# Six PSUM buffers by role for the seven products of a Strassen pair, the seventh product issued behind the next pair's first, and eight early loads at the start of attention

## The chip, the cores and the metric

The kernel runs on one core of one Trainium2 chip. The metric is device time in microseconds (us) of the whole program. The times of before are three timed runs; the profile is one further execution, taken by the hardware profiler, with its own time.

## The reference, cut to what matters

A decoder block with two branches over 2048 positions and 1024 channels, all in float32:

```python
h = rms_norm(x, g_norm) * (1 + scale) + shift
proj = h @ w_in                                     # 1024 x 8192
x_rnn, z_rnn, q, k, v, z_attn, g_r, g_a = split(proj)
xc = causal_depthwise_conv(x_rnn); hr = rg_lru(xc)  # a gated linear recurrence over positions
y_rnn  = (hr * silu(z_rnn)) @ w_out_rnn
o      = dilated_attention_mixture(rope(q), rope(k), v)
y_attn = (o * silu(z_attn)) @ w_out_attn
merged = sigmoid(g_r + b) * y_rnn + sigmoid(g_a + b) * y_attn
x = rms_norm(x + gate * (merged @ w_o), g_final)
```

## The kernel before

Every float32 operand of a matrix product is split into a high part `h` (float32r) and a remainder `l`, and a product is three matmuls, `h*h + h*l + l*h` (`mm3`, L148). ScalarE (ACT) makes the high part, GpSimd (POOL) or VectorE (DVE) the low part.

The program has these stages. Positions are handled in two halves, f = 0 and f = 1, of two 512-column chunks each.

- **Values** (`values_half`, L645): the columns of `w_in` for v, and the building of the right-hand operands B11, B21, B12, B22, T1 to T4 (`build`, L447, transposes on TensorE (PE) into a PSUM tile of the pool `pg`).
- **Pairs** (`strassen`, L312): 28 pairs of 128 output rows in each half. A pair is a 2 x 2 block product done with seven block products in place of eight, each of 4 x 3 = 12 matmuls of 128x512. In order of the code they are X (B11), Z (T2), W (T3), V (T1), X again (B21), W again (T4), V again (B22). X, W and V are written twice: the second product of each accumulates onto the first in the same PSUM tile. In between the first content is read: u1 = X (ACT, L338), u2 = Z + u1 (DVE, L339), u3 = W + u2 (DVE, L344), and `done(1, 1, V, u3)`. After the second products come `done(0, 0, X)`, `done(1, 0, W, u2)` and `done(0, 1, V, u2)`. Each `done` begins with `total` (L379), one ACT copy or one DVE addition out of PSUM (L385), and goes on with what belongs to the output: `recurrent` (L674: convolution taps, gates on PE, exponentials, root, scan), `gate_pairs` (L879), `plain_pairs` (L853) or `rotated_pairs` (L833: the rotary part of q and k, which needs tables Ct and St that `rotary_tables` makes at the start of that section). The 28 pairs are 22 of recurrent, gate and plain kind, then 2 rotated, then 4 plain ones.
- In half 0 the left operands (seven sums of blocks of `w_in`) are loaded, added on DVE (L254 to L262), split on ACT and POOL (`split_s`, L198) into a ring of seven tiles S0 to S6, used, and stored to DRAM (`sD`); in half 1 they are read back, one DMA of 512 KB for each product (`load_next`, L282), into the same ring.
- The steps of `recurrent` are not issued at once. `steps_after` (L216) puts each behind a number of further products: in units of products after the pair's `done(0, 0)`, tap 0, taps 1, split 2, gates 4, sigmoids 5, decay 6, exponentials 7, root 8, scan 9, finish and store 10; for the second column chunk 7 later.
- **Attention** (L973 on): heads in an order written out by slots. Matmuls of the output products (`steps`, L1306) fill PE between its parts; they begin the stage. Their right operands are 8 tiles yh/yl of each chunk, made by `split_y` (L1339) from rows of `yaT`. For the first chunk, k = 0 to 3 are loaded during the last pair into R0 to R3 (`load_next`, L294), and k = 4 to 7 after the split of k - 4 has released its R tile (L1371).
- **Output** (L1457 on): the last projection and the final norm.

Within the stages up to attention a scheduler decides the order in which each engine's instructions stand; `tc.high_priority()` marks the reads of PSUM. The rows of an engine stand in that order, and a row that waits holds up the rows behind it. Attention's order is that of the code.

PSUM has eight banks. Before, five are in the pool `pj` and rotate over whatever asks next (four tiles a pair, two tiles a step of values), three in `pg` (transposes of `build`, the gates of `recurrent`, the rotary tables).

In the profile the products of the pairs are the group `pj<-T,S` at L146, the DVE totals `ev`, `t`, `zs` or `xr` `<-pj,u` at L385, by the output that they belong to.

## Time and profile before

| what | value |
|---|---|
| three timed runs | 2347.64, 2355.68, 2358.10 us (median 2355.68) |
| profiled execution, its own time | 2350.21 us |
| its span, first to last instruction | 2348.4 us |
| granted TensorE clock, mean | 0.986 |
| busy share of the span | PE 95%, DVE 58%, ACT 51%, POOL 41% |

A row of a timeline reads: start, duration, engine, line, operation, output tile <- input tiles, count, and in brackets the idle time of that engine just before it and what ended it. A row of waits reads: who waited, for whom, us in total, times, longest. A row of windows reads: the stretch, its length, then busy us and the number of instructions of each engine, the granted clock of PE, the busy share of the DMA engines and GB/s. "PE busy" comes with modelled ends, so the number of matmuls in a stretch says more than its busy time.

### The profile page before, as it was taken

How to read it: one execution, taken by the hardware profiler on the slowest of the kernel's cores; microseconds unless marked ns; L12 is line 12 of the kernel's file. 1: busy time of each engine (PE TensorE's matmuls, PEld its weight loads, DVE VectorE, ACT ScalarE, POOL GpSimd, SP SyncE). 2: the span in 40 equal slices, each digit the busy share in tenths (PEclk: the TensorE clock that was granted, in tenths of full speed). 3: DMA queues.
4: the chain of work that ended last, by engine and by line, in shares of the span. 5: the costliest groups of instructions: out<-in, count | busy, mean ns of one | idle time of the engine just before them, and what ended most of it. 6: DMA issues, size and time to landing. Idle time of an engine off the chain costs nothing.

```text
span 2348.4 us, 34038 instructions
## 1 busy us (share of the span) xinstructions
PE 2228.8 (95%) x11397; PEld 1875.8 (80%) x11397; DVE 1353.7 (58%) x2457; ACT 1202.0 (51%) x2386; POOL 954.5 (41%) x734
## 2 busy tenths in 40 slices
PE   6999999999999999999999999899989998989998
PEld 6897777777777898778888877788879887978887
DVE  6837666766676534444444472366667778657443
ACT  4636656666643535555444410466667777634111
POOL 1356655655555533333111120355556656433000
PEclk9999999999999999999999999999999999999999
DMA  7376877677878659899676678888888878799532
GB/s 259 99 226 220 275 248 258 244 247 247 258 259 251 220 175 338 305 310 330 215 234 224 232 241 257 267 257 274 263 247 262 240 244 251 221 315 291 173 119 96
DMA packets 427331, 569.19 MB, mean 242 GB/s; under 512 B 71990, under 2 KB 292882, under 8 KB 426132
## 3 DMA queue, kind: packets, MB, share of 16 engines
q1 hardware_dynamic: 389316, 447.27, 61.4%
q10 hardware_dynamic: 37648, 119.70, 13.4%
q8 instruction: 90, 1.47, 0.3%
q14 instruction: 85, 0.70, 0.1%
q0 software_dynamic: 192, 0.05, 0.0%
HBM read 355.08 MB, written 211.82 MB: 241 GB/s over the span
## 4 chain that ended last, share of the span: by engine, by line
PE 62%; DMA 9%; DVE 8%; ACT 5%; issue 4%; POOL 2%; SPq 1%; ACTq 1%; DVEq 0%; POOLq 0%
PE pj L146 43%; PE pq L146 7%; PE sc L146 4%; PE o L146 4%; DMA R<-in_w_in_dram 1%; PE pg L146 1%; PE pT L1154 1%; POOL S L160 1%; DMA S<-sD 1%; PE pT L1167 1%; DMA vraw<-vN 1%; ACT L742 1%; DMA gw<-in_w_mod_dram 1%; DVE xc L718 1%; DMA R<-yaT 1%
## 5 line engine op out<-in xcount | busy, mean ns | idle before, releaser
L146 PE MATMUL pj<-T,S 128*128 128x512 f32 x4704 | 1120.6, 398 | 29.8 <-DVE ev L385 20.1
L146 PEld LDWEIGHTS pj<-T,S 128*128 128x128 f32 x4704 | 888.7, 190 | 249.6 <-DVE ev L385 27.0
L146 PE MATMUL pj<-yh,S 128*128 128x512 f32 x1024 | 370.5, 407 | 12.4 <-ACT yh L154 6.7
L160 POOL TENSOR_TENSOR S<-R,S 128x512 fp32r<-128x512 f32 x168 | 244.8, 1469 | 277.7 <-ACT S L200 105.7
L146 PEld LDWEIGHTS pj<-yh,S 128*128 128x128 f32 x1024 | 195.1, 191 | 49.6 <-ACT yh L154 7.1
L146 PE MATMUL pj<-yl,S 128*128 128x512 f32 x512 | 202.8, 396 | 1.0 <-POOL yl L160 0.6
L1070 ACT ACTIVATE pp<-pp,st 128x256 f32<-128x256 f32 (+3 forms) x256 | 133.9, 524 | 110.9 <-DVE st L1069 110.2
L146 PE MATMUL pj<-S,T 128*128 128x256 f32 x1152 | 160.7, 295 | 4.4 <-ACT S L154 1.3
L146 PEld LDWEIGHTS pj<-S,T 128*128 128x128 f32 x1152 | 150.1, 199 | 5.9 <-POOL S L160 1.6
L160 POOL TENSOR_TENSOR S<-s,S 128x512 fp32r<-128x512 f32 x84 | 112.2, 1338 | 73.9 <-ACT S L200 38.6
L163 DVE TENSOR_TENSOR ptl<-pT,pth 128x384 fp32r<-128x384 f32 (+1 forms) x160 | 97.9, 628 | 66.8 <-ACT pth L154 64.7
L1134 ACT ACTIVATE pp<-pp,M 128x256 f32<-128x256 f32 (+3 forms) x256 | 118.0, 522 | 9.0 <-DVE M L1258 9.0
L718 DVE SCALAR_TENSOR_TENSOR xc<-xr,par,xc 128x512 f32<-128x512 f32 x96 | 83.9, 874 | 65.5 <-ACT xc L712 64.9
L1069 DVE CUSTOM_DVE_ANT_0 pp<-sc,msk 128x256 f32<-128x256 f32 (+3 forms) x256 | 104.9, 449 | 26.8 <-PE sc L146 24.4
L339 DVE TENSOR_TENSOR u<-pj,u 128x512 f32<-128x512 f32 x56 | 38.4, 686 | 135.9 <-PE pj L146 70.1
L160 POOL TENSOR_TENSOR kq<-kraw,kq 128x512 fp32r<-128x512 f32 (+1 forms) x64 | 101.1, 1590 | 29.0 <-ACT kq L154 29.0
L146 PEld LDWEIGHTS pj<-yl,S 128*128 128x128 f32 x512 | 98.0, 191 | 15.5 <-POOL yl L160 1.1
L160 POOL TENSOR_TENSOR vh<-vraw,vh 128x256 fp32r<-128x256 f32 (+1 forms) x64 | 67.2, 1050 | 102.8 <-ACT vh L154 80.1
L698 POOL TENSOR_TENSOR zs<-zs,sg 128x512 f32<-128x512 f32 x32 | 47.3, 1477 | 142.2 <-ACT sg L694 135.8
L146 PE MATMUL pq<-oh,mh 128*128 128x512 f32 x256 | 99.2, 391 | 1.4 <-ACT mh L154 1.4
L146 PE MATMUL pq<-ol,mh 128*128 128x512 f32 x256 | 99.7, 390 | 0.0
L146 PE MATMUL pq<-oh,ml 128*128 128x512 f32 x256 | 99.3, 390 | 0.0
(301 smaller groups left out, 3898.7 us busy)
## 6 DMA issues: line engine op xcount, KB each, us to landing
sD<-S ACTq DMA_DIRECT2D x196, 512.0 KB, 3.7
S<-sD SPq DMA_DIRECT2D x196, 512.0 KB, 5.3
S<-wD SPq DMA_DIRECT2D x99, 512.0 KB, 5.4
R<-in_w_in_dram SPq DMA_DIRECT2D x136, 256.0 KB, 4.1
wD<-s ACTq DMA_DIRECT2D x64, 256.0 KB, 5.8
T<-in_w_mod_dram SPq DMA_DIRECT2D x8, 1024.0 KB, 11.7
vN<-ev SPq DMA_DIRECT2D x64, 128.0 KB, 2.1
zaT<-ev SPq DMA_DIRECT2D x32, 256.0 KB, 5.8
```

Of the source, the lines that this page charges most:

```text
L146: last_mm[0] = nc.tensor.matmul(o, lhsT=l, rhs=r, start=st, stop=sp, **kw).ins
L160: nc.gpsimd.tensor_tensor(o, i, h.bitcast(F32), ALU.subtract)
L163: return nc.vector.tensor_tensor(o, i, h.bitcast(F32), ALU.subtract).ins
L339: nc.vector.tensor_tensor(u2[:], Z[:], u1[:], ALU.add)
L698: (2, lambda: nc.gpsimd.tensor_tensor(z[:], z[:], sg[0][:], ALU.mult))))
L718: nc.vector.scalar_tensor_tensor(xc, xr[:, i : i + CH], cw(i), xc, ALU.mult, ALU.add)
L742: nc.scalar.activation(a, y, AF.Exp, scale=-1.0)
L1069: nc.vector.tensor_tensor_reduce(pdst, s_ps, mask, 1.0, 3e38, ALU.add, ALU.min, m_)
L1070: nc.scalar.activation(pdst, pdst, AF.Exp, bias=m_, scale=-1.0, accum_out=l_)
L1134: nc.scalar.activation(pp, pp, AF.Copy, scale=w)
L1154: nc.tensor.transpose(pt[:, c0 + j * P : c0 + (j + 1) * P], pp[i][:, k * P : (k + 1) * P], ident)
L1167: nc.tensor.transpose(pt[:, c * P : (c + 1) * P], pp[:, half * P : (half + 1) * P], ident)
```

## The change

1. **Roles.** `pj` has six single-purpose banks: X with two buffers, Z, W, V, Y with one each. `pg` has two. The T4 product no longer accumulates onto W: it goes into Y, and `done(1, 0)` adds u3 (which holds W) in place of u2. Two products are still accumulated onto a first content: X and V.
2. **The seventh product** (V, B22) and its `done(0, 1)` are put into a list `behind` and issued after the first product of the next pair (or at the end of a section). Its left operand is taken from the ring in the old order (`take`), so in half 1 the loads wait until the oldest tile of the ring has been used (`used`).
3. **Steps of `recurrent`**: root 9 (was 8), scan 11 (was 9), finish and store 12 (was 10), with a third buffer for `zs` and a second for `xc`.
4. **`build`** puts every third transpose tile into Y when no pair is running; the tiles of values cycle through X, Z, W, X, V.
5. **Attention's first eight inputs**: k = 4 to 7 of the first chunk come in one DMA of 1 MB into a tile `T` of the pool `hp`, issued when the second product of the last pair is done; the four loads after `split_y` are gone.
6. Small: defaults in the `done` closures (they now run after the loop has moved on), the even operands built in the last plain pairs one product later, `finish_late` runs only its own list.

```diff
-            loaded.append(t)
+            loaded.append((n, t))
...
+            if k == 1:
+                t = T(hp, [P, KH, CH], F32, "T", bufs=14)
+                nc.sync.dma_start(t[:], yaT[KH * P :, :CH].rearrange("(k p) j -> p k j", p=P))
+                for i in range(KH):
+                    Y0[True, 0, KH + i] = t[:, i, :]
...
-        def prod(ps, b, first, last):
-            s = loaded.pop(0) if f else next(ops)
+        def take():
+            return (f, *loaded.pop(0)) if f else (f, 7 * x, next(ops))
+
+        def prod(ps, b, first, last, op=None):
+            f, i, s = op or take()
...
             if f:
-                load_next()
+                used.add(i)
+                while n_loaded[0] - NS in used:
+                    load_next()
             run_late(n_prod[0])
 
-        X = T(pj, [P, CH], F32, "pj")
+        X = T(pj, [P, CH], F32, "X", bufs=2)
         prod(X, "B11", True, False)
-        Z = T(pj, [P, CH], F32, "pj")
+        last_product()
+        Z = T(pj, [P, CH], F32, "Z")
         prod(Z, "T2", True, True)
...
-        W = T(pj, [P, CH], F32, "pj")
-        prod(W, "T3", True, False)
+        W = T(pj, [P, CH], F32, "W")
+        prod(W, "T3", True, True)
...
-        V = T(pj, [P, CH], F32, "pj")
+        V = T(pj, [P, CH], F32, "V")
         prod(V, "T1", True, False)
         done(1, 1, V, u3)
         prod(X, "B21", False, True)
         done(0, 0, X, None)
-        prod(W, "T4", False, True)
-        done(1, 0, W, u2)
-        prod(V, "B22", False, True)
-        done(0, 1, V, u2)
+        Y = T(pj, [P, CH], F32, "Y")
+        prod(Y, "T4", True, True)
+        done(1, 0, Y, u3)
+        op = take()
+
+        def last():
+            prod(V, "B22", False, True, op)
+            done(0, 1, V, u2)
+        behind.append(last)
...
-    pj = pools.open("pj", bufs=5, space=PSUM)
-    pg = pools.open("pg", bufs=3, space=PSUM)
+    pj = pools.open("pj", bufs=1, space=PSUM)
+    pg = pools.open("pg", bufs=2, space=PSUM)
...
-        pt = T(pg, [P, 4, P], F32, "pg")
+        n_built[0] += 1
+        pt = T(pj, [P, 4, P], F32, "Y") if spare and n_built[0] % 3 == 0 else T(pg, [P, 4, P], F32, "pg")
...
-            z = zs[j] = T(rp, [P, CH], F32, "zs", bufs=2)
+            z = zs[j] = T(rp, [P, CH], F32, "zs", bufs=3)
...
-                nc.scalar.activation(new("xc"), xr[:, 0:CH], AF.Identity, scale=cw(0),
+                nc.scalar.activation(new("xc", bufs=2), xr[:, 0:CH], AF.Identity, scale=cw(0),
...
-                (8, root), (9, scan), (10, finish), (10, store)))
+                (9, root), (11, scan), (12, finish), (12, store)))
...
             split_y(0, k)
-            if k + 4 < KT:
-                load_y(0, k + 4)
```

The order of instructions shows what this moves. The first place is PE in half 0, in the fourth pair: the first matmul of each product from V's first (T1) to V's second (B22), before. The tile numbers tell the buffers apart; pj_2233 is V, pj_2148 X, pj_2209 W, pj_2337 the next pair's X.

```order
L146 MATMUL pj_2233<-T_975,S_330_2234 128x512 [waits DVE_49]
...
L146 MATMUL pj_2148<-T_155,S_332_2256 128x512 [waits Activation_49]
...
L146 MATMUL pj_2209<-T_981,S_337_2284 128x512 [waits DVE_49]
...
L146 MATMUL pj_2337<-T_153,S_348_2346 128x512 [waits PE_49,Activation_49]
...
L146 MATMUL pj_2233<-T_649,S_339_2310 128x512 [waits DVE_49]
```

The next pair's X has only two of its matmuls ahead of V's second product here. The same place on PE now, up to the next pair's V.

```order
L146 MATMUL V_2236<-T_975,S_333_2237 128x512 [waits DVE_49]
...
L146 MATMUL X_2126<-T_155,S_335_2259 128x512 [waits Activation_49]
...
L146 MATMUL Y_2287<-T_981,S_341_2288 128x512
...
L146 MATMUL X_2316<-T_153,S_349_2325 128x512 [waits Activation_49]
...
L146 MATMUL V_2236<-T_649,S_343_2312 128x512 [waits DVE_49,Activation_49]
...
L146 MATMUL Z_2363<-T_977,S_356_2368 128x512 [waits Activation_49]
...
L146 MATMUL W_2399<-T_979,S_362_2401 128x512 [waits Activation_49]
...
L146 MATMUL V_2425<-T_975,S_367_2426 128x512 [waits DVE_49]
```

A whole product (X_2316) has moved ahead of V's second product, the T4 product waits for nobody, and the next pair's V, in the same bank, now stands two products (and the gates between them) behind.

The second place is DVE in the eighth pair of half 0: the rows from u3 to the scan of `recurrent`, before. L747 and L752 are the arithmetic of root and scan, t and gi tiles of `recurrent`.

```order
L344 TENSOR_TENSOR u_456_2960<-pj_2938,u_451_2935 128x512 [waits DVE_49,PE_49]
L747 SCALAR_TENSOR_TENSOR t_3004<-y_2956,t_3004 128x512 [waits Activation_49]
L752 TENSOR_TENSOR t_3004<-t_3004,gi_2957 128x512 [waits Activation_49,Pool_49]
L385 TENSOR_TENSOR ev_2981<-pj_2962,u_456_2960 128x512 [waits DMAHW4_49,DVE_49,PE_49]
L753 SCALAR_TENSOR_TENSOR y_2956<-a_3003,htail_441,t_3004 128x512 [waits DVE_49]
```

And now (L357 is u3, L784 and L789 are the two rows of `recurrent`, L418 is the total):

```order
L357 TENSOR_TENSOR u_463_2967<-W_2943,u_458_2940 128x512 [waits DVE_49,PE_49]
L784 SCALAR_TENSOR_TENSOR t_3011<-y_2963,t_3011 128x512 [waits Activation_49]
L418 TENSOR_TENSOR ev_2988<-V_2969,u_463_2967 128x512 [waits DMAHW4_49,DMAHW2_49,DMAHW5_49,DVE_49,PE_49]
L789 TENSOR_TENSOR t_3011<-t_3011,gi_2964 128x512 [waits Activation_49,Pool_49]
L790 SCALAR_TENSOR_TENSOR y_2963<-a_3010,htail_441,t_3011 128x512 [waits DVE_49]
```

The row that waits for ACT's square root stood ahead of the total that reads V, and stands behind it now. Among the three rows ahead of V's first total, the square-root row stands in 10 of the 28 pairs of half 0 before and in none now; in half 1 in 10 before and in 9 now.

The third place is the SP queue at the start of attention, before: the last stores of k, the mask, the first keys and queries, and the loads of yaT for k = 4 to 7.

```order
L872 DMA kT<-t_2116_12590 256x1x128 [waits DMAHW3_49]
L981 DMA msk_12618<-in_cst_dram 128x896 [waits DMAHW4_49,PE_49]
L1017 DMA kraw_12675<-kT 128x256 [waits DMAHW5_49]
...
L1018 DMA kraw_12678<-qT 128x256 [waits DMAHW0_49]
L309 DMA R_2121_12625<-yaT 128x512 [waits DMAHW1_49,Pool_49]
...
L309 DMA R_2130_12643<-yaT 128x512 [waits DMAHW4_49,DVE_49]
```

And now: the one load stands 16 rows ahead of the mask, and the second pair of key loads waits for DVE and POOL, the last readers of that tile.

```order
L299 DMA T_12557<-yaT 128x4x512 [waits DMAHW5_49,PE_49]
L310 DMA S_2152_12528<-wD 128x1024 [waits DMAHW6_49,PE_49]
L288 DMA S_2151_12526<-sD 128x1024 [waits DMAHW7_49,PE_49]
...
L1020 DMA msk_12676<-in_cst_dram 128x896 [waits DMAHW5_49,PE_49]
L1056 DMA kraw_12725<-kT 128x256 [waits DMAHW6_49,PE_49]
L1057 DMA kraw_12725<-qT 128x256 [waits DMAHW7_49]
L1056 DMA kraw_12728<-kT 128x256 [waits DMAHW0_49,DVE_49,Pool_49]
```

The four loads of yaT have left the place between the key loads and what follows them.

More of the change, by code (lines that the diff above doesn't have):

```diff
@@ L213, in finish_late @@
         while late:
-            run_late(min(late))
+            for fn in late.pop(min(late)):
+                fn()
     def steps_after(start, steps):
@@ L276, in first_operands @@
             yield t
-    loaded, n_loaded = [], [0]
+    loaded, n_loaded, used = [], [0], set()
     def load_next():
@@ L349, in strassen, with last_product, pj_tile @@
         done(0, 0, X, None)
-        prod(W, "T4", False, True)
-        done(1, 0, W, u2)
-        prod(V, "B22", False, True)
-        done(0, 1, V, u2)
+        Y = T(pj, [P, CH], F32, "Y")
[6 more added lines that the diff above has]
+        behind.append(last)
+    behind = []
+    def last_product():
+        while behind:
+            behind.pop()()
+    pj_tags, n_pj = ("X", "Z", "W", "X", "V"), [0]
+    def pj_tile(shape):
+        tag = pj_tags[n_pj[0] % 5]
+        n_pj[0] += 1
+        return T(pj, shape, F32, tag, bufs=1 + (tag == "X"))
     def output_weights():
@@ L445, in norm_x, with build @@
             nc.vector.tensor_scalar(t, t, ss[:, 1:2], None, ALU.mult)
-    def build(st, names, xs, k, first=False, keep=None):
+    n_built = [0]
+    def build(st, names, xs, k, first=False, keep=None, spare=True):
         hh, hl = B[names[k // KH]]
-        pt = T(pg, [P, 4, P], F32, "pg")
+        n_built[0] += 1
+        pt = T(pj, [P, 4, P], F32, "Y") if spare and n_built[0] % 3 == 0 else T(pg, [P, 4, P], F32, "pg")
         for r in range(4):
@@ L466, in operand, with build_even @@
         B[name] = (slot(), slot())
-    def build_even(st, xs, ks=range(KT), first=False):
+    def build_even(st, xs, ks=range(KT), first=False, spare=True):
         for k in ks:
-            build(st, ("B11", "B21"), xs, k, first)
+            build(st, ("B11", "B21"), xs, k, first, spare=spare)
     def build_odd(st, xs):
@@ L609, in values_by_halves @@
         names = ("B12", "B22") if n % 2 else ("B11", "B21")
-        pss = [T(pj, [P, 2, 256], F32, "pj") for g in range(2)]
+        pss = [pj_tile([P, 2, 256]) for g in range(2)]
         for kh in range(2):
@@ L634, in values @@
         for g in range(2):
-            ps = T(pj, [P, 2, 256], F32, "pj")
+            ps = pj_tile([P, 2, 256])
             for r in range(2):
@@ L835, in rotated_pairs, with rotated @@
         for base, dstT, qs in QK:
-            def rotated(i, j, ps, u):
+            def rotated(i, j, ps, u, dstT=dstT, qs=qs):
                 n = 2 * f + j
@@ L866, in plain_pairs, with plain @@
             for t in range(0, 6, 2):
-                def plain(i, j, ps, u):
+                def plain(i, j, ps, u, t=t, dstT=dstT, qs=qs):
                     n = 2 * f + j
@@ L881, in gate_pairs, with gate @@
             for base, dst, b0 in ((5 * D, zaT, None), (6 * D, grT, C_BG), (7 * D, gaT, C_BG + 8)):
-                def gate(i, j, ps, u):
+                def gate(i, j, ps, u, m=m, dst=dst, b0=b0):
                     n = 2 * f + j
@@ L920, in next_even @@
             operand("B21" if p else "B11")
-        build_even(xp, x0, (p,) if p < 6 else (6, 7))
+        build_even(xp, x0, (p,) if p < 6 else (6, 7), spare=False)
     for f in range(2):
@@ L945, in decoder_block @@
                 n += 1
+        last_product()
         finish_late()
@@ L964, in decoder_block @@
                 for p in range(7):
-                    late.setdefault(n_prod[0] + p + 1, []).append(lambda p=p: next_even(p))
+                    late.setdefault(n_prod[0] + p + 1 + (p > 0), []).append(lambda p=p: next_even(p))
+        last_product()
         finish_late()
```

## The prediction

> **What bounds the kernel now.** I read the page first: the busy shares and the granted clock, to see which engine could set the end at all.
>
> ```profile
> span 2348.4 us, 34038 instructions
> PE 2228.8 (95%) x11397; PEld 1875.8 (80%) x11397; DVE 1353.7 (58%) x2457; ACT 1202.0 (51%) x2386; POOL 954.5 (41%) x734
> ```
>
> TensorE (PE) is busy for 95% of the span and no other engine for more than 58%. So a microsecond that PE does not wait is a microsecond of the end, unless something else becomes late. The windows by stage then say where PE loses time. First one stretch without any wait, as a yardstick, then half 0's recurrent, gate and plain pairs (153 to 645), the rotary section with its last pairs (645 to 754), half 1's pairs (879 to 1338, 1338 to 1463) and the first 37 us of attention.
>
> ```profile
> 1100.00:1200.00 100.00, 100.00 (x431) 80.77 (x430) 47.11 (x60) 50.90 (x79) 17.25 (x14) 1.00 0.68 230
> 153.00:645.00 492.00, 464.31 (x1949) 368.55 (x1948) 324.76 (x344) 297.71 (x491) 296.44 (x212) 0.99 0.74 253
> 645.00:754.00 109.00, 102.19 (x437) 81.40 (x436) 78.11 (x133) 37.94 (x68) 58.38 (x40) 0.97 0.80 254
> 879.00:1338.00 459.00, 454.72 (x1946) 366.34 (x1946) 203.73 (x255) 232.68 (x364) 114.03 (x85) 1.00 0.81 272
> 1463.00:1500.00 37.00, 29.31 (x134) 23.78 (x133) 10.34 (x31) 10.99 (x28) 10.12 (x10) 0.86 0.77 237
> ```
>
> The yardstick is 100 / 431 = 0.232 us a matmul, so a product of 12 lasts 2.78 us. Half 0's pairs hold 1949 matmuls, worth 452 us, and last 492: some 40 us are lost. Half 1's first stage loses 459 - 1946 x 0.232 = 7.5 us, and attention's start (a few of its matmuls are short) 6 us or a little more. The change can win little anywhere else.
>
> The waits of PE, asked for stage by stage, name the releasers. The first five rows are 153 to 645, the next one 879 to 1338, the next 1338 to 1463, the last three 1463 to 1500.
>
> ```profile
> PE pj L146 <- DVE ev L385: 15.9, 12, 2.7
> PE pg L146 <- POOL xl L160: 4.8, 4, 2.5
> PE pg L146 <- ACT xh L154: 2.7, 3, 1.2
> PE pj L146 <- DVE u L344: 2.3, 2, 1.8
> PE pj L146 <- DVE zs L385: 1.8, 1, 1.8
> PE pj L146 <- DVE ev L385: 4.2, 2, 2.9
> PE pj L146 <- DMA S<-sD: 2.4, 2, 1.7
> PE pj L146 <- ACT yh L154: 6.7, 1, 6.7
> PE pj L146 <- POOL yl L160: 0.6, 1, 0.6
> PE pj L146 <- DVE yl L163: 0.5, 1, 0.5
> ```
>
> The rows with L385 or L344 are PE waiting to accumulate a second product onto a bank whose first content DVE has not yet read: V's B22 behind `done(1, 1)`, and W's T4 behind u3. One of them in the timelines of DVE and PE, in the eighth pair:
>
> ```profile
> 328.76 0.69 DVE L747 SCALAR_TENSOR_TENSOR t<-y,t 128x512 f32<-128x512 f32 x1 [1.56 <-ACT y L743]
> 331.29 0.69 DVE L752 TENSOR_TENSOR t<-t,gi 128x512 f32<-128x512 f32 x1 [1.84 <-ACT t L748]
> 331.90 0.68 DVE L385 TENSOR_TENSOR ev<-pj,u 128x512 f32<-128x512 f32 x1
> 332.64 1.67 PE L146 MATMUL pj<-T,S 128*128 128x512 f32 x6 [1.16 <-DVE ev L385]
> ```
>
> V's first product had ended at 322.65. The total that reads it (331.90) stands behind two rows of the recurrence that wait for ACT, the last for the root, and PE waits with it.
>
> Such waits also cost clock. Three of them in PE's timeline, and then windows: the 3.4 us around or behind each, the 10.2 us around attention's wait, and 3.4 us at the pair just shown.
>
> ```profile
> 376.00 9.72 PE L146 MATMUL pj<-T,S 128*128 128x512 f32 x34 [2.23 <-DVE ev L385]
> 983.43 29.80 PE L146 MATMUL pj<-T,S 128*128 128x512 f32 x120 [2.85 <-DVE ev L385]
> 244.30 8.20 PE L146 MATMUL pj<-T,S 128*128 128x512 f32 x34 [2.61 <-DVE ev L385]
> ...
> 376.60:380.00 3.40, 3.40 (x10) 2.63 (x9) 3.40 (x6) 3.35 (x7) 0.73 (x1) 0.50 0.74 275
> 984.20:987.60 3.40, 3.40 (x9) 2.63 (x8) 2.86 (x3) 1.55 (x4) 1.43 (x1) 0.51 0.64 233
> 244.30:247.70 3.40, 3.40 (x15) 2.76 (x16) 3.40 (x5) 3.37 (x6) 0.13 (x1) 1.00 0.54 209
> 1468.80:1479.00 10.20, 5.01 (x11) 3.65 (x12) 2.48 (x2) 4.41 (x7) 6.04 (x5) 0.50 0.77 243
> 328.80:332.20 3.40, 2.68 (x7) 1.57 (x5) 1.56 (x3) 3.35 (x5) 1.64 (x2) 0.50 0.87 321
> ```
>
> At full clock (244.30) 3.4 us hold 15 matmuls; behind two of the three waits they hold 9 or 10 at a clock of 0.50. So some waits of 2 to 3 us are followed by 5 or 6 lost matmuls, 1.1 to 1.4 us, and others by none. The Trainium skill ("TensorE: Matmul & The Clock Gate", Part 1: The HAM clock gate) has the clock fall only after at least one idle window of about 3.4 us; by that alone no wait of the pairs would cost clock, and the forecast below would be 2325.5 in place of 2322. The two rows at 0.50 say otherwise, and I go by them.
>
> **The change part by part.**
>
> *Half 0's pairs.* T4 into its own bank Y removes u3's wait (2.3). The seventh product moved behind the next pair's first puts three products, 8.35 us, between V's two products where there were two, 5.57. The longest wait there is 2.7, under the 2.78 added: all of 15.9 + 1.8 goes, if DVE is no later than now. With the two half-clock stretches (376.60: 15 - 10 matmuls; 328.80: 2.68 busy us are worth 11.6, it held 7) another 10 x 0.232 = 2.2. Together 22.2. The 7.5 us of waits on xl and xh before the gates stay: their lags are unchanged, and `pg` with two banks still holds one part's two gate tiles.
>
> What comes new is that V has one bank: the next pair's T1 must wait until `done(0, 1)` has read it, with Z and W between, again 5.57 us, or 7.0 where six gate matmuls stand there. I followed these reads through half 0's 22 pairs of this stage (end of V's second product to the end of the total that reads it): 2.1 to 9.0 us, the longest in the second pair, where the product's last matmul ended at 193.74:
>
> ```profile
> 200.35 1.77 DVE L753 TENSOR_TENSOR_SCAN y<-a,htail,t 128x512 f32<-128x512 f32 x1
> 202.04 0.66 DVE L385 TENSOR_TENSOR ev<-pj,u 128x512 f32<-128x512 f32 x1
> ```
>
> With these latencies unchanged, the excess over 5.57 or 7.0 adds up to 4.7 us, and the first reads of V that last over 8.35 (8.6, 8.6, and 9.9 for the row at 331.90) add 2.2. But the later root, scan and finish take the row that waits for the root from in front of V's first total in all ten pairs where it stood there, the second `xc` lets a tap go before the last part is done, and the seventh product comes 2.8 us later, when DVE has had time to catch up. Bounds 0 and 6.9; I take 2.5. Net gain 19.7.
>
> *The rotary section.* The wait of 25 us here is no wait of PE: the fourth output of the first rotated pair needs a t0 buffer (three in half 0), which comes free when the tables are there.
>
> ```profile
> 641.73 35.36 PE L146 MATMUL pj<-T,S 128*128 128x512 f32 x151 [0.39 <-DVE ev L385]
> 691.32 0.68 DVE L385 TENSOR_TENSOR t<-pj,u 128x512 f32<-128x512 f32 x1
> 706.80 10.18 PE L146 MATMUL pj<-T,S 128*128 128x512 f32 x36 [2.63 <-ACT t L827]
> ```
>
> V's second product ended some 106 matmuls into the first row, at 666.6; the read ended at 692.0. With one bank V the next pair's T1 can't start before that. But PE's new order has put that T1 behind 93 other matmuls and three groups of transposes, 23 us. I take 0; bounds: 3.7 won (706.80 and a half-clock stretch of 1.1 as above), 20 lost (25.4 - 5.57).
>
> *Half 1's pairs.* 4.2, and 984.20's 5.7 matmuls, 1.3: 5.5 us gone. The root's row still stands ahead of V's total, but 2.9 us late against 2.8 more. The reads of V's second product take at most 7.0 us in this stage, so 0 to 1.5 new; I take 0.5. Net 5.0. The ring of loads now runs one product shorter, 2.8 us; PE waited 2.4 us for `S<-sD` at the end of half 1, and I charge 1 (0 to 3).
>
> *Attention's start.* ACT splits k = 0 to 3, then waits for R tiles to be released, loaded and to land; SP issues those loads behind mask and keys:
>
> ```profile
> 1458.22 2.18 ACT L154 ACTIVATE yh<-R 128x512 fp32r<-128x512 f32 x4
> 1467.86 1.80 SPq L309 DMA_DIRECT2D R<-yaT  x4
> 1472.75 0.63 ACT L154 ACTIVATE yh<-R 128x512 fp32r<-128x512 f32 x1 [0.88 <-DMA R<-yaT]
> 1473.43 0.80 PE L146 MATMUL pj<-yh,S 128*128 128x512 f32 x1 [6.68 <-ACT yh L154]
> ```
>
> With the load 16 rows earlier on SP, all eight splits run from 1458. This removes 6.7 + 0.6 and the clock: 5.01 busy us are worth 21.6 matmuls and held 11, 2.5 us. Together 9.8. What is late next: the low parts, 0.5 us as now, and the keys, since the second key tile waits for the splits of k = 6 and 7 and PE comes to the scores 10 us sooner. Bounds 5 and 9.8; I take 8.5.
>
> *The rest.* Two `pg` banks and every third transpose in Y touch the start of the program, where PE waits for a chain of loads and DVE anyway: 1 us lost (1 won to 3 lost). The tile cycle of values keeps five buffers; closures, `finish_late` and the later even operands cost nothing: the same instructions, beside pairs that PE fills.
>
> Sum: 19.7 + 0 + 5.0 - 1 + 8.5 - 1 = 31.2 us off the profiled 2350.2 (its span and 1.8 around it): 2319.0. The median of the timed runs is 5.5 above the profiled execution; I add half of that and say 2322.
>
> **The rivals.**
>
> *The wait moves (0.13).* DVE is late for reasons that buffers don't touch, and with one V the wait turns up at the next pair's T1. For it: the 9.0 us above, and DVE at 66% in this stage. Against it: the cleared order on DVE. Half 0 and 1 then win nothing: 2322 + 19.7 + 5.0 = 2347. The Trainium skill ("TensorE: Matmul & The Clock Gate", section "HAM oscillation — how this bites in real kernels") tells of a kernel that PSUM double-buffering gave no further gain. By that the pairs would win nothing either; the wait rows above show that here a bank is waited for.
>
> *The rotary section pays (0.07), slower.* The single V holds PE up wherever a rotated output waits for its t0 buffer: 25.4 - 5.57 = 19.8 in half 0's first rotated pair, and two more reads of that kind are as late, in its second and in half 1's second:
>
> ```profile
> 716.49 0.69 DVE L385 TENSOR_TENSOR t<-pj,u 128x512 f32<-128x512 f32 x1
> 1391.78 0.67 DVE L385 TENSOR_TENSOR t<-pj,u 128x512 f32<-128x512 f32 x1
> ```
>
> V's second products had ended at 701.4 and 1379.4, so 15.8 and 13.0 us, 10.2 and 7.4 over 5.57. With 2.5 us of half clock for each, as behind attention's wait, that is 45 us: 2367, where half a per cent over the median begins. It makes the kernel slower than before from 34 us on. Against it: the order has moved those T1 products back; 93 matmuls stand in the first gap.
>
> *Attention gives its part back (0.10).* PE comes to the keys too early, or DMA, 0.77 busy there, is late: 2322 + 8.5 = 2330.
>
> **How the numbers follow.** The forecast has 0.65. The best ends of its terms add up to 42.2, the worst to 14.3 with 4 of the rotary section's 20, so 2311 to 2339. Attention's rival has 0.10, the moved wait 0.13, the rotary section 0.07; 0.05 lies below the forecast, where the gate waits go too (7.5, to 2303). The range, 2306 to 2346, takes in the first two, half of the moved wait and part of what lies below. Half a per cent, 11.8 us, is about what a measurement of this kernel can tell from no change, so faster needs less than 2343.9. The forecast, attention's rival and the part below lie there: 0.80; the moved wait within, 0.13; the rotary section I count as slower, 0.07.
>
> **What would show it.** Right: no wait of PE on a DVE total or u3 over 1 us between 153 and 645, over 2000 matmuls in 492 us there, clock 1.00 in that stage, no wait on yh at attention's start. Wrong: rows of PE waiting for the second total of V ahead of T1, a PE wait of over 5 us in the rotary section, or PE waiting on kq after 1475.

## The result, and the profile after

The changed kernel takes 2340.39 us (median of nine runs, 2335.58 to 2350.24) against 2354.84 before (nine runs): a ratio of 0.9946, 95% interval 0.9928 to 0.9963. It is 14.5 us faster where 33 were forecast. The direction and the place of more than half of the gain were right; the largest term of the sum, 19.7 us in half 0's pairs, came out at nothing.

The page of the changed kernel's profiled execution (its own time 2345.26 us), then the five stretches that the prediction worked with:

```profile
span 2343.2 us, 33925 instructions
PE 2232.0 (95%) x11397; PEld 1876.0 (80%) x11397; DVE 1359.2 (58%) x2457; ACT 1201.4 (51%) x2387; POOL 951.4 (41%) x734
```
```profile
153.00:645.00 492.00, 462.29 (x1924) 367.01 (x1923) 328.37 (x341) 292.19 (x486) 297.29 (x208) 0.97 0.72 249
645.00:754.00 109.00, 99.82 (x416) 79.27 (x415) 74.87 (x133) 38.14 (x68) 54.78 (x39) 0.94 0.79 249
879.00:1338.00 459.00, 455.36 (x1954) 366.52 (x1954) 205.38 (x255) 233.78 (x365) 108.70 (x85) 1.00 0.81 273
1338.00:1463.00 125.00, 123.40 (x534) 97.95 (x533) 56.44 (x104) 19.01 (x33) 17.19 (x12) 1.00 0.83 272
1463.00:1500.00 37.00, 36.22 (x182) 30.03 (x180) 12.08 (x44) 13.91 (x41) 12.53 (x13) 1.00 0.89 281
```

PE is busy for 95% of the span as before; the page shows no difference but the span, 5.2 us less. In the windows read the matmul counts. Half 0's pairs held 1949 before and hold 1924 now: no gain at all. The rotary section holds 416, not 437: 21 x 0.232 = 4.9 us lost. Half 1's pairs hold 8 more, and attention's first 37 us hold 182, not 134. The rotary section's loss does not last: up to 879, where half 1's pairs begin, PE is busy for 223.76 us before (first row) and 223.57 now.

```profile
645.00:879.00 234.00, 223.76 (x1349) 197.45 (x1348) 136.53 (x230) 98.88 (x174) 118.39 (x82) 0.98 0.71 226
645.00:879.00 234.00, 223.57 (x1343) 197.01 (x1342) 136.15 (x231) 100.06 (x176) 114.93 (x82) 0.97 0.72 225
```

The waits of PE in the same stages (153 to 645, then 645 to 754, then 879 to 1338, then 1338 to 1463, then 1463 to 1500):

```profile
PE pg L146 <- ACT xh L154: 16.2, 5, 5.8
PE V L146 <- ACT t L785: 6.5, 4, 3.7
PE V L146 <- DVE ev L418: 3.3, 2, 2.6
PE V L146 <- ACT S L200: 2.3, 1, 2.3
PE pg L146 <- POOL xl L160: 1.2, 3, 0.5
PE pg L846 <- DVE rep L844: 5.5, 2, 5.1
PE Y L146 <- DVE t L418: 2.1, 1, 2.1
PE X L146 <- ACT t L864: 1.2, 1, 1.2
PE pg L146 <- ACT xh L154: 3.0, 1, 3.0
PE V L146 <- DVE ev L418: 0.6, 1, 0.6
PE V L146 <- DMA S<-sD: 1.6, 1, 1.6
PE pj L146 <- DVE yl L163: 0.5, 1, 0.5
```

V's waits in half 0 fell from 15.9 + 1.8 to 6.5 + 3.3 + 2.3, and u3's 2.3 are gone. The waits ahead of the gate products, on xh and xl, rose from 7.5 to 17.4. The sum of all is 27.5 us before and 29.5 now: about what left V came back at the gates, and the new waits cost clock too. Behind those of 5.83, 5.27 and 3.72 us stand 3.4 us at a clock of 0.50 with 9 matmuls in place of 15:

```profile
225.20:228.60 3.40, 3.40 (x9) 2.46 (x9) 1.05 (x1) 1.97 (x6) 3.40 (x4) 0.50 0.77 296
471.40:474.80 3.40, 3.40 (x9) 2.63 (x9) 0.75 (x1) 0.94 (x4) 3.40 (x3) 0.50 0.30 120
641.60:645.00 3.40, 3.40 (x9) 2.63 (x9) 3.33 (x3) 2.88 (x6) 1.28 (x1) 0.50 0.86 251
```

The half clock lasts longer than these 3.4 us, and it also follows waits of 2.58 us (339.02) and 2.82 us (537.83). Over all five stretches PE ran for 24.1 us at 0.50 with 58 matmuls where 104 would fit, by an estimate 46 x 0.232 = 10.7 us lost. Before there were three such stretches in half 0's pairs, 12.1 us with 31 matmuls where 52 would fit, 4.9 us.

The profiled execution is one of the longer of the nine, and its stages understate the gain. One execution also differs from the next. In half 0's pairs the rows of PE and of DVE stand in one and the same order in the traces of the changed kernel and of e3 and e4 below, and they hold 1924, 1942 and 1943 matmuls; before, e1 and e13 are one order too, and hold 1949, 1936 and 1935. So a difference of under 20 matmuls between two traces of this stage decides nothing, and none are won in it.

The longest of the new waits, in the timelines of PE, DVE and ACT of the changed kernel:

```profile
216.04 2.94 PE L146 MATMUL Z<-T,S 128*128 128x512 f32 x12
224.81 1.22 PE L146 MATMUL pg<-xh,gh 128*128 128x512 f32 x2 [5.83 <-ACT xh L154]
...
213.91 2.20 DVE L790 TENSOR_TENSOR_SCAN y<-a,htail,t 128x512 f32<-128x512 f32 x1
216.03 1.72 DVE L255 TENSOR_TENSOR s<-R,R 128x512 f32<-128x512 f32 x1
217.68 2.08 DVE L795 TENSOR_TENSOR zs<-y,zs 128x512 f32<-128x512 f32 x1
219.69 1.70 DVE L258 TENSOR_TENSOR R<-R,R 128x512 f32<-128x512 f32 x1
221.31 0.74 DVE L755 SCALAR_TENSOR_TENSOR xc<-xr,par,xc 128x512 f32<-128x512 f32 x1
...
224.13 0.63 ACT L154 ACTIVATE xh<-xc 128x512 fp32r<-128x512 f32 x1 [0.76 <-DVE xc L755]
```

PE has nothing left but the gate products. Their input xh needs three taps on DVE, and DVE does the scan, two sums of left operands and finish first, without a pause. In PE's order the gate products of a part stand 48 matmuls behind the product that its X total reads (44 to 51), before as now. These 48 took 11.3 us before, without a wait among them, and take 11.8 now. PE's rows before, from the gates of the part ahead of it to the same place:

```profile
200.20 0.50 PE L146 MATMUL pg<-xh,gh 128*128 128x512 f32 x1 [0.88 <-ACT xh L154]
203.24 0.79 PE L146 MATMUL pg<-xl,gh 128*128 128x512 f32 x1 [2.54 <-POOL xl L160]
...
205.54 21.40 PE L146 MATMUL pj<-T,S 128*128 128x512 f32 x84
227.58 0.73 PE L146 MATMUL pg<-xh,gh 128*128 128x512 f32 x2 [0.64 <-ACT xh L154]
```

There PE lost 3.4 us at the earlier gates and had 0.64 to wait at these. Now it loses nothing at the earlier ones, waits 2.30 us for a left operand (201.50), and then 5.83 here. From the first gates of half 0 to the last it is 447.5 us before (180.34 to 627.81) and 449.7 now (174.88 to 624.55): the gates come no faster, whatever PE waits for on the way.

### The profile page after: what moved, and what is told of

It is laid out like the page before. It is cut to its first block, busy times and chain, and to the rows that moved or that the text cites. A ratio compares the mean times of both kernels' runs of the same rounds, so it can differ in the third digit from the quotient of the medians.

```text
span 2343.2 us, 33925 instructions
## 1 busy us (share of the span) xinstructions
PE 2232.0 (95%) x11397; PEld 1876.0 (80%) x11397; DVE 1359.2 (58%) x2457; ACT 1201.4 (51%) x2387; POOL 951.4 (41%) x734
## 4 chain that ended last, share of the span: by engine, by line
PE 53%; DMA 7%; DVE 4%; ACT 3%; issue 2%; POOL 2%; SPq 1%; ACTq 0%; POOLq 0%; DVEq 0%
PE pj L146 11%; PE pq L146 7%; PE X L146 6%; PE V L146 6%; PE sc L146 4%; PE o L146 4%; PE W L146 4%; PE Z L146 4%; PE Y L146 3%; PE pT L1193 1%; DMA wD<-s 1%; PE pg L146 1%; PE pT L1206 1%; DMA vN<-ev 1%; DMA S<-sD 1%
## 5 line engine op out<-in xcount | busy, mean ns | idle before, releaser
L146 PE MATMUL V<-T,S 128*128 128x512 f32 x1344 | 336.8, 399 | 14.5 <-ACT t L785 6.5
L146 PE MATMUL X<-T,S 128*128 128x512 f32 x1344 | 333.1, 396 | 1.2 <-ACT t L864 1.2
L146 PEld LDWEIGHTS V<-T,S 128*128 128x128 f32 x1344 | 254.0, 190 | 79.0 <-ACT t L785 8.7
L146 PEld LDWEIGHTS X<-T,S 128*128 128x128 f32 x1344 | 253.0, 189 | 62.3 <-ACT t L864 2.1
L146 PE MATMUL W<-T,S 128*128 128x512 f32 x672 | 173.1, 402 | 0.0
L146 PE MATMUL Y<-T,S 128*128 128x512 f32 x672 | 168.3, 398 | 2.1 <-DVE t L418 2.1
L146 PE MATMUL Z<-T,S 128*128 128x512 f32 x672 | 167.9, 398 | 0.0
L146 PEld LDWEIGHTS W<-T,S 128*128 128x128 f32 x672 | 129.8, 193 | 32.3 <-issue 0.9
L146 PEld LDWEIGHTS Y<-T,S 128*128 128x128 f32 x672 | 126.7, 189 | 33.2 <-DVE t L418 2.5
L146 PEld LDWEIGHTS Z<-T,S 128*128 128x128 f32 x672 | 127.6, 190 | 30.4
```

Of the source, the lines that this page charges most:

```text
L146: last_mm[0] = nc.tensor.matmul(o, lhsT=l, rhs=r, start=st, stop=sp, **kw).ins
```

## The experiments

All numbers of one table first. The ratio is to the kernel before, timed beside it on the same chip; the medians come from several chips, so compare the ratios. The waits are those of PE from 153 to 645 us added up, with those ahead of a pair's products in brackets (the rest stands ahead of the gates); the last column counts the matmuls in that stretch.

| kernel | median us | ratio, 95% interval | waits us (products) | matmuls |
|---|---|---|---|---|
| before | 2354.84 | 1 | 27.5 (20.0) | 1949 |
| changed | 2340.39 | 0.9946, 0.9928 to 0.9963 | 29.5 (12.1) | 1924 |
| e1 early load alone | 2343.73 | 0.9962, 0.9946 to 0.9978 | 28.0 (18.9) | 1936 |
| e2 gates later | 2354.55 | 1.0008, 0.9991 to 1.0024 | 31.7 (21.0) | 1906 |
| e3 old lags | 2339.49 | 0.9948, 0.9929 to 0.9967 | 26.5 (9.8) | 1942 |
| e4 taps at high priority | 2340.42 | 0.9937, 0.9915 to 0.9958 | 27.3 (11.0) | 1943 |
| e5 root behind total | 2349.23 | 0.9992, 0.9979 to 1.0004 | 28.4 (5.9) | 1932 |
| e6 scan behind taps | 2345.51 | 0.9972, 0.9961 to 0.9982 | 28.3 (12.6) | 1931 |
| e7 both orders | 2346.39 | 0.9981, 0.9965 to 0.9996 | 27.4 (7.9) | 1933 |
| e10 seventh in place | 2352.68 | 1.0011, 0.9998 to 1.0025 | 29.2 (26.7) | 1940 |
| e11 no root | 2336.74 | 0.9942, 0.9922 to 0.9963 | 26.9 (17.1) | 1931 |
| e12 early load, no root | 2351.86 | 0.9997, 0.9981 to 1.0012 | 30.6 (25.5) | 1899 |
| e13 two gate banks | 2356.14 | 1.0019, 1.0005 to 1.0033 | 32.6 (22.9) | 1935 |
| e14 Y from the gate ring | 2343.46 | 0.9962, 0.9944 to 0.9980 | 29.4 (12.2) | 1926 |
| e15 half 1 only | 2342.36 | 0.9964, 0.9943 to 0.9984 | 30.6 (27.4) | 1925 |
| e16 no sums | 2312.78 | 0.9832, 0.9800 to 0.9863 | 7.2 (4.5) | 2063 |
| e17 early load, no sums | 2311.62 | 0.9834, 0.9802 to 0.9866 | 4.3 (1.9) | 2081 |
| e18 deferral alone | 2341.02 | 0.9956, 0.9937 to 0.9975 | 29.6 (24.1) | 1929 |
| e19 one sum on POOL | 2335.70 | 0.9931, 0.9912 to 0.9950 | 25.7 (4.5) | 1955 |
| e20 finish on POOL | 2336.91 | 0.9935, 0.9916 to 0.9953 | 27.0 (10.1) | 1950 |

**Attention's part, and the new lags.** e1 is the kernel before with the early load alone; e3 the changed kernel with `(8, root), (9, scan), (10, finish), (10, store)`.

> The kernel before with attention's early load alone (eight inputs loaded early, nothing else). All theories: the two waits on yh and yl at attention's start (6.7 and 0.6 us) and the half clock behind them go; 2354.8 less 8.5 (5 to 9.8), so about 2346. If it gains nothing, the 14.5 us of the whole change came from the pairs after all; if it gains 14, the pairs gave nothing at all.

> The changed kernel with the old lags of root, scan, finish and store (8, 9, 10, 10). Theory L (the later scan and finish came to stand in front of the taps on DVE, and so made xh late): the waits on xh fall from 16.2 us in half 0 to under 6, and the time to about 2328. Theory G: the gate products stand where they stood, 48 matmuls behind X; waits on xh 16 within 4 us, the waits on V rise by 0 to 6; 2340 to 2348.

e1 wins 8.9 us (0.38% of 2353.1, interval 5.2 to 12.7): the term of 8.5 was right, and it is more than half of the whole gain. What the rest of the change adds, 0.16% or 3.8 us, is not clear of the noise, since the two intervals overlap. e3 is the changed kernel's equal, with waits of 14.4 us on xh. With the old lags the rows of PE and of DVE come to stand in the same order in half 0, so the lags do nothing there, and theory L falls.

**Room ahead of the gates.**

```diff
-                (0, tap), (1, taps), (2, split), (4, gates), (5, sigmoids), (6, decay), (7, exponentials),
-                (9, root), (11, scan), (12, finish), (12, store)))
+                (0, tap), (1, taps), (2, split), (4 + late0, gates), (5 + late0, sigmoids), (6 + late0, decay),
+                (7 + late0, exponentials), (9, root), (11, scan), (12, finish), (12, store)))
```

`late0` is 1 for a pair's first part. e4 puts `with tc.high_priority():` around tap, taps and split.

> The changed kernel with the steps gates to exponentials of a recurrent pair's first part one product later, so that 60 matmuls and not 48 stand between X's second product and the gate products. Theory G (a fixed chain: X's total, three taps and the split need more than four products; the removed wait on V lay inside that stretch and hid it): each wait on xh shrinks by 2.8 us, from 16.2 us in half 0 and 3.0 in half 1 to about 6 together, some half-clock windows go with them; 2340.4 less 10 to 16, so 2324 to 2330. Theory D (DVE and ACT can't deliver faster, whatever PE does in between): the waits turn up at V or at S instead; 2340 within 4 us.

> The changed kernel with tap, taps and split at high priority: DVE does the taps ahead of the left operands' sums and of finish, and the order of PE too has 60 matmuls ahead of the gate products. Theory G: no wait on xh over 1 us in half 0 (16.2 now), at least what e2_gates_later gains, 2322 to 2330. Theory D: left operands come later instead, PE waits for S; 2340 within 4 us.

With 60 matmuls in front, e2's waits on xh did fall, to 4.3 us. But V's rose, and the kernel lost the whole gain: theory G, a chain that only needs more room, falls.

```profile
PE V L146 <- DVE ev L418: 11.6, 4, 4.1
PE V L146 <- ACT t L785: 6.5, 3, 3.6
PE pg L146 <- POOL xl L160: 6.4, 4, 2.8
PE pg L146 <- ACT xh L154: 4.3, 2, 2.3
PE V L146 <- ACT ev L932: 2.9, 1, 2.9
```

e4 was a miss as an experiment: in half 0 the rows of PE and of DVE stand as in the changed kernel, the taps behind the sums and finish and 48 matmuls, not 60, ahead of the gates; only a few rows of ACT and POOL have moved. It is the changed kernel once more, with 14.5 us of waits on xh and the same time, and decides nothing between G and D.

**DVE's order.** In e5 and e7 the root's row is queued behind V's first total, in e6 and e7 the scan behind the taps:

```diff
+                with tc.issue_after(v_total[0]):
+                    nc.vector.scalar_tensor_tensor(t, v["y"][:], 1.0, t, ALU.add, ALU.mult)
...
+                with tc.issue_after(last_tap[0]):
+                    nc.vector.tensor_tensor(t, t, v["gi"][:], ALU.mult)
```

> The changed kernel with the root's row on DVE queued behind the total that reads V's first product (the order on DVE alone changes). Theory O (PE is held by the order of rows on DVE: the total of V behind the root's row, the taps behind scan and finish, each a holder of its own): the waits on V for a DVE total or for the ACT row ahead of it (9.8 us in half 0) fall under 3, the waits on xh stay (16 within 4); 2340 less 5 to 9, so 2331 to 2335. Theory D (DVE and ACT can't deliver the pair faster in any order): the waits on xh grow by what V's lose; 2340 within 4 us.

> The changed kernel with the scan (and finish behind it) queued on DVE behind the last taps written before it, so that at the two narrow spacings of half 0 (two recurrent pairs with one pair between) the taps come first. Theory O: the two waits of 5.8 and 5.3 us on xh fall under 2.5 each and their half-clock windows go; xh in half 0 under 10 us; 2340 less 6 to 12, so 2328 to 2334. Theory D: what the gates win comes back as waits on V or S; 2340 within 4 us.

> Both orders of the two kernels beside this one. Theory O: the two gains add, 2319 to 2328, and PE's waits from 153 to 645 come to under 15 us (29.5 now). Theory D: 2340 within 4 us.

In e5 the two groups of V's waits for a total or for the row ahead of it, 9.8 us, fell to 3.3. The waits on xh rose from 16.2 to 20.6, and the kernel became slower. But more than DVE's order moved in e5 and e7: ACT's rows did too, and from 153 to 645 ACT loads its tables 63 times, not 51, at 1.283 us each, and is busy for 307 and 308 us, not 292. That is a second reason for their loss. e6 has 51 loads: its waits on xh fell to 12.6 us, the others rose from 13.3 to 15.7, and it became no faster. So theory O falls by e6, and e5 and e7 do not contradict it. D, that DVE and ACT deliver no faster in another order, has the direction, but its 2340 within 4 us was too kind to all three.

**The parts of the change.** e10 issues the seventh product at the end of its own pair (`last()` in place of `behind.append(last)`). e13 is the kernel before with `bufs=2` for `pg`. e14 takes Y from `pg` with three banks. e18 keeps the deferral, accumulates T4 onto W as before and has three gate banks. e15 has all of the old arrangement in half 0 and the new one in half 1.

> The changed kernel with the seventh product run at its old place, at the end of its own pair (all else as changed: Y for T4, two banks for the gates, the lags, the early load). By the prediction's working V's waits come back in half 0 and half 1: 2340.4 plus 20, near 2360. By the traces so far (a wait removed at V returned at the gates in half 0, while half 1 kept its gain): half 0 within 4 us of the changed kernel, half 1 4 to 8 longer; 2343 to 2350.

> The kernel before with two gate banks in place of three and nothing else (one bank left unused). Theory T (the tables' transposes in the rotary section need the third bank; with two the later tables and so the first rotated outputs come late): 3 to 7 us longer, all of it between the last recurrent pairs of half 0 and the values of half 1; 2356 to 2360. If the bank is spare, as the prediction had it: 2353 within 3 us.

> The changed kernel with Y taken from the gate banks' ring, three banks in all for gates, transposes and T4. Theory T: the tables' transposes stand close together again, the rotary section gives back its 4 us, 2333 to 2338; the half-0 pairs as in the changed kernel, or 0 to 3 longer where T4 now takes turns with the gates. If the section's loss has another cause: 2340 within 3 us.

> The seventh product behind the next pair's first, with T4 accumulated onto W as before, no bank Y and three gate banks (so X twice, Z, W, V and three), the lags and the early load. Theory R with the rotary loss put down to the two gate banks: 2332 to 2338. If the rotary loss comes from the one V: as the changed kernel, 2340 within 3.

> The five-bank ring, the three gate banks and the seventh product in its place in half 0, as before; the changed buffers and order in half 1 alone; the early load. Theory R (in half 0 the rows of DVE, ACT and POOL set the pace, buffers only choose where PE waits; the rotary section loses 4 us to the change; half 1 wins 5): half 0 and its rotary section as before, half 1 about 5 shorter, attention 9: 2334 to 2339. If the deferral wins in half 0 too: over 2343.

e10 lost all: the roles with the seventh product in its old place are 0.9946 to 1.0011 worse, 15 us, and 11.5 us worse than the early load alone (0.9962 to 1.0011). So the deferral is worth 15 us here, and the rest of the change costs most of that. Only about half of the 15 us is found in the traces: 3.5 in half 1 (1939 matmuls from 879 to 1338, not 1954) and 3.6 from 645 to 879 (PE busy for 220.01 us, not 223.57); half 0 has no part in it (1940 and 1924). e18 wins no more than the changed kernel, and its waits moved again, from V to W's first content:

```profile
PE W L146 <- DVE u L357: 14.9, 15, 1.9
PE W L146 <- DVE ev L417: 6.5, 6, 2.7
PE pg L146 <- ACT xh L154: 5.5, 2, 4.2
```

In the rotary section, 645 to 754, a ring of five banks lets 433 to 442 matmuls through (e13 433 with two gate banks, before 437, e1 441 and e15 442 with three). With banks by role it is fewer: 404 in e18, 410 in e10, 416 in the changed kernel, 423 in e14. It is no strict rule: e11 and e20, by role, hold 433 and 431, and e12, with the ring, 422. So theory T falls: three gate banks (e14, e18) do not bring the matmuls back, and two of them in e13 cost 4 x 0.232 = 0.9 us by an estimate, less than executions differ by. The fixed roles cost 14 to 33 matmuls there, 3 to 8 us, of which not all lasts: from 645 to 879 PE is busy for 223.0 to 225.3 us in before, e1, e13 and e15, and for 220.0 to 223.6 in the changed kernel, e3, e4, e10, e14 and e18. Which role does it, the one V or another, was not tried. e13 is 4.2 us slower as a whole, the time that T forecast, but where was not found. e14 is no better than the changed kernel (0.9962), and e15 wins back the rotary section, but its 2342 is no better either.

**The length of the recurrence.** e11 (from the changed kernel) and e12 (from e1) lack one line, `nc.scalar.activation(t, t, AF.Sqrt)`.

> The changed kernel with the square root on ACT left out (the row and its table load; the rows of DVE all stay), so a part's recurrence is some 2.1 us shorter from gates to scan. Theory C (PE is held in half 0 by the length of the recurrence's chain, gates to scan to the next part's taps and split, wherever the wait shows up): PE's waits from 153 to 645 fall from 29.5 us to under 15, its half-clock windows with them, and the time by 10 to 20, to 2320 to 2330. Theory D (DVE's rows are too many for the pair): DVE has the same rows, 2340 within 4 us.

> The kernel before with attention's early load and without the square root on ACT: what the same shortening is worth with the old buffers. Theory C: the total of V stands behind a root that comes 2.1 us sooner, so most of the 14.4 us of waits on V in half 0 go without any buffer; 2343.7 less 6 to 14, so 2330 to 2338. If the buffers were what held PE (the prediction's working), the waits on V stay above 10 us and the time at 2340 or more.

Neither gained. e11's waits went the other way, from the gates (9.8 of 26.9 us) to the products (17.1); e12 came out 8 us slower than e1, with 1899 matmuls where e1 has 1936; why was not found. Theory C falls.

**DVE's rows.** So far all sixteen kernels had waits between 26.5 and 32.6 us. The groups of DVE's rows in the changed kernel, 153 to 645, show what none of the busy shares does; ahead of the second bar busy us and mean ns, behind it the idle time in front of the rows:

```profile
L263 DVE TENSOR_TENSOR s<-R,s 128x512 f32<-128x512 f32 x22 | 31.9, 1451 | 17.4 <-DMA R<-in_w_in_dram 12.8 <-POOL S L160 4.6
L258 DVE TENSOR_TENSOR R<-R,R 128x512 f32<-128x512 f32 x22 | 30.3, 1377 | 0.4
L255 DVE TENSOR_TENSOR s<-R,R 128x512 f32<-128x512 f32 x21 | 21.0, 1002 | 27.7 <-DMA R<-in_w_in_dram 27.7
L256 DVE TENSOR_TENSOR s<-s,R 128x512 f32<-128x512 f32 x22 | 16.3, 740 | 47.1 <-POOL S L160 47.1
```

The four sums of a pair's left operands are busy for 99.5 us, and DVE stands idle for another 92.6 in front of them, waiting for raw blocks and for POOL's splits. Every total and tap queued behind waits with them. Together that is 192 of the 492 us on the engine that PE is waiting for. e16 and e17 take the sums out and put raw blocks in their place, so their products are not those of the block product:

```diff
-        nc.vector.tensor_tensor(s1[:], a21, a22, ALU.add)
-        nc.vector.tensor_tensor(s2[:], s1[:], a11, ALU.subtract)
-        yield split_s(s2[:])
-        nc.vector.tensor_tensor(a21, a11, a21, ALU.subtract)
+        yield split_s(a22)
...
-        nc.vector.tensor_tensor(s2[:], a12, s2[:], ALU.subtract)
-        yield split_s(s2[:])
+        yield split_s(a12)
```

> The changed kernel with the four sums of each pair's left operands (DVE, half 0 alone) left out, the raw blocks taken in their place; PE, ACT and POOL keep their rows. Theory R: PE's waits from 153 to 645, 27 to 33 us in all kernels so far, fall under 15; half 0 is 10 to 25 shorter, 2316 to 2330. If DVE's rows don't set the pace: 2340 within 4 us.

> The kernel before with the early load and without the same four sums of each pair. Theory R: half 0 is shorter by about as much as in e16_no_sums, without any new buffer: 2343.7 less 10 to 25, so 2319 to 2334. If what holds PE here is the bank of V alone: the waits on V stay above 10 us, 2340 within 4.

The window from 153 to 645 of e16, with the new buffers, and its longest waits there:

```profile
153.00:645.00 492.00, 482.06 (x2063) 386.80 (x2061) 268.55 (x317) 314.32 (x520) 294.13 (x221) 1.00 0.79 272
```
```profile
PE V L146 <- DVE ev L412: 3.6, 2, 2.4
PE pg L146 <- ACT xh L154: 2.4, 2, 1.2
```

The same of e17, with the old ones:

```profile
153.00:645.00 492.00, 485.98 (x2081) 390.05 (x2080) 251.81 (x303) 316.02 (x521) 304.59 (x222) 1.00 0.80 274
```
```profile
PE pg L146 <- ACT xh L154: 1.4, 2, 1.3
PE pj L146 <- DVE zs L385: 1.1, 1, 1.1
```

The waits collapse to 7.2 and 4.3 us, the clock is 1.00, and by the ratios 27 us are won over the changed kernel and 30 over e1. The two medians lie 1.2 us apart. With the sums gone, the old five-bank ring holds PE no more than the new roles: theory R holds, and that the bank of V held PE falls. The same bank waits that the change was aimed at went without any new bank. From the first gates to the last it is 417.3 us in e16 (174.03 to 591.35) and 418.3 in e17 (178.64 to 596.91), against 447.5 before. The two do not say which part of the sums holds PE: DVE's 99.5 us, the idle time in front of them, or the way of a left operand from its block over the sum to the split, which is shorter without the sum.

**A row from DVE to POOL.** e19 computes `a11 - a21` with `nc.gpsimd.tensor_tensor`, e20 the product of finish.

> The changed kernel with one of the four sums of each pair (a11 - a21, 28.6 us of DVE from 153 to 645) on POOL. Theory R, DVE's rows alone set the pace of half 0: leaving out all four (97.9 us) won 27.6 us, so a part of 28.6 / 97.9 wins about 8, 2330 to 2336. Theory R2, the loop over DVE and POOL sets it (POOL is busy for 297 us of the 492 and its rows of 1.3 to 1.7 us slow DVE's): what DVE is spared comes back on POOL; 2340 within 4, or longer.

> The changed kernel with the last product of the recurrence (finish, 21.2 us of DVE from 153 to 645) on POOL, in both halves. Theory R: 21.2 / 97.9 of 27.6, about 6 won; 2331 to 2337. Theory R2: 2340 within 4, or longer.

Medians of 2335.7 and 2336.9, 3.5 and 2.6 us better than the changed kernel by their ratios, under half of R's 8 and 6, and within the intervals no difference. Both medians lie at the upper end of R's ranges and close to R2's, so R and R2 are not separated. They are the shortest medians of kernels with the whole computation here, and faster than before beyond doubt; that they beat the changed kernel is not shown (e4, the changed kernel once more in half 0, has 0.9937). In e19 DVE's busy time in the stretch fell from 328 to 314 us, half of the moved row's 30.3, and POOL's rose from 297 to 328. The two together were not tried.

## Why the prediction was right or wrong

- **Half 0's pairs, 19.7 us: wrong, and this is the step that failed.** The prediction said "all of 15.9 + 1.8 goes, if DVE is no later than now" and "The 7.5 us of waits on xl and xh before the gates stay: their lags are unchanged". The waits ahead of the products fell only from 20.0 to 12.1 us, and the gates' 7.5 became 17.4, with the lag in products unchanged. The lag's time was not what shrank: at the gates with the new waits of 5.83, 5.27 and 2.82 us the 48 matmuls ahead took 11.3, 13.4 and 11.3 us before and take 11.8, 12.0 and 11.4 now. The gate inputs come at a pace of their own, and a PE that waits less elsewhere stands at the gates earlier. Half clock costs an estimated 10.7 us, not 4.9. The deeper error stands a step earlier: PE's waits were read as the fault of the bank named in the row. e16 and e17 show that in half 0 the sums of left operands, in DVE's queue, set the pace, with new banks or without, and the prediction never looked at the idle time in front of DVE's rows. Whether DVE's own time or what the sums wait for counts more stays open.
- **The order on DVE: half right.** The scan's first row did leave its place in front of V's first total, but the root's row, which also waits for ACT, stayed there (325.68, then the total at 327.00, and PE waited 2.07). By e3 the lags had no part in it.

```profile
325.68 1.40 DVE L784 SCALAR_TENSOR_TENSOR t<-y,t 128x512 f32<-128x512 f32 x1 [1.92 <-ACT y L780]
327.00 0.68 DVE L418 TENSOR_TENSOR ev<-V,u 128x512 f32<-128x512 f32 x1
327.83 3.02 PE L146 MATMUL V<-T,S 128*128 128x512 f32 x12 [2.07 <-ACT t L785]
```

- **The rotary section, 0 (3.7 won to 20 lost): within its bounds.** 4.9 us are lost by 754, 0.2 by 879. The rival's mechanism, a T1 held up behind V's read, does not appear as a wait; the loss shows as waits on `rep` (5.5), on a total (2.1) and on X (1.2).
- **Half 1's pairs, 5.0 less 1: right.** Here there are no sums on DVE (205 of 459 us busy). In the two stretches 8 and 6 more matmuls fit, 14 x 0.232 = 3.2 us, and against e10 (1939 in 879 to 1338) the deferral wins 15, 3.5 us. Other traces agree for 879 to 1338: e3, e4 and e15 hold 1962, 1962 and 1959 with the new arrangement, e1 and e13 1927 and 1946 with the old one. The charge of 1 for the shorter ring was not needed: the wait for `S<-sD` fell from 2.4 to 1.6. Even here the waits on V went from 4.2 to 0.6 us while 3.0 came up on xh.
- **Attention's start, 8.5: right**, 8.9 in e1. All eight splits run without a pause (1457.78 to 1462.05), and PE waits 0.5 us for yl; the wait on kq that the prediction named as a sign of failure did not come.

- **The start, 1 lost: not seen.** The first pair begins at 148.9 us, about as early as in e1 (147.5), which has the old start; before it was 153.2.
- **Its own signs.** It asked for no wait on a DVE total over 1 us, over 2000 matmuls and a clock of 1.00 in half 0: it got 2.6 us, 1924 and 0.97. The rotary wait over 5 us, a sign of failure, came (5.1).
- **The rivals.** Nearest was the moved wait (0.13): "DVE is late for reasons that buffers don't touch". Its reason fits what the runs show; its place was wrong, the gates and not the next T1. Its 2347 was 6.6 us too long where the forecast's 2322 was 18.4 too short. The rule it was weighed against, the Trainium skill's "TensorE: Matmul & The Clock Gate", section "HAM oscillation — how this bites in real kernels", where PSUM double-buffering gave no further gain, agrees with this case: the new banks won no matmuls in half 0 (1949 before, 1924 now), and half 1's gain came with the deferral (e10, with the banks and without it, 1939, before 1946).

## What to carry to other kernels

A wait row names who came last, not what sets the pace: before buying a bank for it, look at the queue of the engine named, at its busy time and at the idle time in front of each of its groups, and at what else PE waits for between the same two points. If the sum of an engine's waits in a stage stays the same while their places change, look for the cause in a supplier's queue; take rows away from the supplier, as a probe, before rearranging buffers. Lags counted in products are no guarantee of time: they help only if the supplier delivers at that pace, and an engine that no longer waits in one place is early at the next. And before a difference between two traces is read, two traces of the same order of rows show how far executions differ: here by 19 matmuls of 1943.

## What the runs showed of the hardware

The same sum on DVE, of two SBUF tiles, takes 0.68 us alone and 1.72 while POOL is at work:

```profile
705.64 0.68 DVE L255 TENSOR_TENSOR s<-R,R 128x512 f32<-128x512 f32 x1
...
216.03 1.72 DVE L255 TENSOR_TENSOR s<-R,R 128x512 f32<-128x512 f32 x1
```
```profile
215.63 1.58 POOL L735 TENSOR_TENSOR zs<-zs,sg 128x512 f32<-128x512 f32 x1 [0.59 <-DMA sD<-S]
```

POOL's row ends at 217.21, and the sum ends 0.54 us later, at 217.75. The Trainium skill ("SBUF — State Buffer", section "SBUF: two separate sides") has the two engines share a pair of ports under an exclusive lock: a DVE operation with two SBUF inputs waits for the whole of a POOL instruction that reads SBUF and began first. These rows agree. The mean of the sums at L258 is 1.377 us, twice the lone 0.68, so by an estimate about half of their 30.3 us is POOL's doing. It may also bound what e19 and e20 can win, since a row moved to POOL is one more that DVE's may wait for; no run shows how much.
